# One decoder layer on one core: loads of a second input moved ahead, a gate's small products moved behind larger ones, and the last tile computed half by half

## Chip, core and metric

The kernel runs on one NeuronCore of a Trainium2 chip. The metric is device time of one execution in microseconds (us). A profile is one further execution recorded by the hardware profiler; times inside it count from the start of its span.

## What is computed

One layer of a hybrid decoder for a prompt of 1024 tokens and 8 samples of 4 tokens (32 columns beside the 1024). Cut to what matters here:

```python
u = rmsnorm(x, norm_pre); proj = u @ w_in                  # all mixer inputs and gates
a = hgrn2_branch(...) @ w_pa; b = swa_branch(...) @ w_pb
m = sigmoid(ga) * a + sigmoid(gb) * b
y = m @ w_o
x = x + rmsnorm(y, norm_post)
e = (p @ w_ple) * sigmoid(x @ w_ple_gate)                  # p: the second input, 256 wide
x = x + e
```

The change lies in the last three lines: in how `p` (`p_prompt`, `p_sample`) is loaded and transposed while `m @ w_o` runs, and in `x @ w_ple_gate` with the output that follows it.

## The kernel before, in words

Activations lie with channels on partitions and tokens along the free dimension. A weight matrix of 1024 columns is worked through in four tiles, each of two blocks of 128 output columns (`across`: blocks p and p+4). float32 operands are split in a high and a low part (`wh`, `wl` for weights, H.., L.. for activations), so that one block product takes three matmuls of 128x512.

`pair_gemm` (L403) computes one such tile. For w_pa, w_pb and w_o it uses a seven-product scheme with "plain" groups for the two contraction blocks that are left over: products P1, P5, P6, P3, P7, P2, P4 of 9 matmuls each, and four plain groups (`plain`, L432) of 6, 87 matmuls in all. They accumulate in three PSUM banks (tile name `g`) which rotate. Product P2 takes the bank that the first plain group had filled, and that bank is free only when VectorE has added it into the tile `p5` (L497). P7 reads the activation variant T3, P2 the variant B21, P4 the variant T4. The variants of the next stage's input are made by `build` (L1459) on VectorE and ScalarE during the first tile of that stage: L1487 subtracts, L1488 rounds to the high part, L1489 makes the low part. T4 is the last; it is made in the tile `ts` with buffer tag `t12`.

The 32 sample columns take another way: `sample_products` (L387) multiplies in 16 small matmuls (L391) and copies the result out on ScalarE (`part`, L394); `sample_outputs` (L397) turns it with four small matmuls (L399), which wait for that copy.

The gate's tiles are of kind "plain" (L456): for each of the two blocks (`j`) both token halves (`t`, 512 columns each) are accumulated in two banks, 36 matmuls, then a plain group of 6 for each half. For j = 0 the sample products and the sample outputs stand between the 36 matmuls and the first plain group. After each half `ep_o` (L1713) works on ScalarE (sigmoid, L1717) and VectorE (L1718, L1719), and after the second half `turn_out` (L1694) is queued: transposes on TensorE (`os` for the samples, `op` for four blocks of 128 tokens), a copy on ScalarE (L1706) and the output DMA.

Order of work. TensorE runs in the order in which the program is written; the order on VectorE and ScalarE, and that of the DMAs on the queue of SyncE (SP), is set by a scheduler. Work beside the matmuls is written as generators in queues; `tick` (L213) is called once in so many matmuls (3 in the stages of w_pa, w_pb and w_o, 6 in the gate), advances the first entry of each queue, and a `yield n` lets n ticks pass. A DMA waits on SP in order: what stands behind a DMA whose buffer is not yet free waits too.

`turn_p` (L1568) transposes p. It starts when the variants of `m` are built (that is, written in the program), takes the tile `pw` of six places with the tag `t12` that `ts` had, and for each of nine blocks issues the load, lets four ticks pass, transposes twice on TensorE (`ppp`, L1578), and splits the result (L1581 on ScalarE, L1582 on VectorE).

Of the kernel before, what the change touches and what calls it, by code (L numbers as in the profile page):

```python
# [121 lines left out]
def tile_decoder_step(ctx: ExitStack, tc: tile.TileContext, x_prompt, x_sample, state_hgrn, cache_k, cache_v,  # L122
# [280 lines left out]
    def pair_gemm(W, X, eps, quantum=QUANTUM, late=False):  # L403
# [53 lines left out]
        if W.kind == "plain":  # L457
            for j in range(2):
                ps = [bank(banks[0]), bank(banks[1])]
# [14 lines left out]
                if j == 0:  # L474
                    sample_outputs(gs, part, eps)
                for t in range(2):
                    plain(ps[t], j, t, False)
                    eps[j](HT * t, slice(HT * t, HT * t + HT), ps[t])
# [1089 lines left out]
    def turn_p():  # L1568
        yield until(("built", id(xm)))
        pw = rt.tile([P, 6, 256], F32, name="pw", tag="t12")  # L1570
        for i in range(9):
            r = P if i < 8 else 32
            pt = pw[:, i % 6, :]
            DM.dma_start(pt[:r], p_prompt[0, 0, i * P:(i + 1) * P, :] if i < 8 else p_sample[0].rearrange("b t d -> (b t) d"))
            yield 4
            b = fps.tile([P, 512], F32, name=f"ppp{i}", tag="xp", bufs=3)
            for k in range(2):
                T.transpose(b[:, k * P:k * P + r], pt[:r, k * P:(k + 1) * P], ident[:r, :r])  # L1578
            bv = b[:, :256].rearrange("p (k t) -> p k t", k=2)[:, :, :r]
            sl = slice(i * P, i * P + r)  # L1580
            S.copy(pH[:, :, sl], bv)  # L1581
            V.tensor_tensor(pL[:, :, sl], bv, pH[:, :, sl], op=ALU.subtract)  # L1582

# [110 lines left out]
    def turn_out(i):  # L1694
        on = op_.tile([P, 9, P], F32, name=f"out{i}", tag="out", bufs=3)
        last = i == KT - 1
        for lo, hi in ((8, 9), (0, 4), (4, 8)):
# [7 lines left out]
            else:  # L1705
                S.copy(on[:, lo:hi, :], b.rearrange("p (j c) -> p j c", j=4))  # L1706
                if last or hi == 8:
                    s = lo if last else 0
                    DM.dma_start(y_prompt[0, s * P:hi * P, i * P:(i + 1) * P].rearrange("(n p) c -> p n c", p=P), on[:, s:hi, :])
            yield 1  # L1710

    for p, W in enumerate(gate_pairs):
        def ep_o(i):  # L1713
            def ep_(ci, sl, ps):
                sg = ctile()[:, :ps.shape[-1]]
                e = eS[:, i, :] if ci == NP else eP[i][ci // HT]
# [3 lines left out]
                if ci == HT:  # L1720
                    enqueue(turn_out(i), 2)
            return ep_

        pair_gemm(W, x1, [ep_o(i) for i in across[p]])
# [28 lines left out]
```

## Time and profile before

| | |
|---|---|
| device time, median of 3 runs | 1540.57 us (1536.43 to 1541.49) |
| the profiled execution's own time | 1533.76 us |
| its span, first to last instruction | 1531.7 us |
| TensorE busy | 1480.7 us, 97% |
| VectorE busy | 1131.8 us, 74% |
| ScalarE busy | 737.6 us, 48% |
| DMA | 85 GB/s mean |

The time of the profiled execution is its span and some 2 us around it. TensorE (PE in the rows) is busy nearly throughout, so what counts is where it stands still, and where its clock is lower. Rows name a line of the kernel, the engine, and output<-input; what stands in square brackets is idle time of that engine just before, and who ended it. [...] The stages that matter here: the tiles of w_pb up to 1282 us, of w_o from there to 1381, the projection of p from 1381 to 1415 with the residual beside it, the gate from 1415 on.

### The profile page before, as it was taken

To read this page: it belongs to the slowest core of one execution; us is meant where nothing else is said; L and a number is where in the kernel's file an instruction comes from. 1 tells how busy PE (TensorE), PEld (TensorE's weight loads), DVE (VectorE), ACT (ScalarE), POOL (GpSimd) and SP (SyncE) were. 2 spreads that over 40 slices of the span, in tenths; PEclk is the share of its full clock that TensorE was granted. 3 is DMA by queue.
4 is the path that set the end of the run, shared out by engine and by line. 5 is a ranking of instruction groups with operands and counts; after the bars stand their busy time and mean duration, and the time that the engine had idled before them with its cause. 6 is when DMAs were issued, how large, how long until landed. Compare 5 with 4: busy or idle time off the path is not lost.

```text
span 1531.7 us, 27146 instructions
## 1 busy us (share of the span) xinstructions
PE 1480.7 (97%) x10013; PEld 1168.8 (76%) x10013; DVE 1131.8 (74%) x2627; ACT 737.6 (48%) x1913; POOL 141.5 (9%) x131
## 2 busy tenths in 40 slices
PE   8889999999999999999999999999999997999998
PEld 7767787877778877777777777777777776789776
DVE  7778868686868777776788788875886979547532
ACT  6334444545354444445555555644634426556332
POOL 2243111202020202013000000000000000000000
PEclk9999999999999999999999999999999999999999
DMA  5212131212122121212222211124665621214221
GB/s 188 70 31 84 43 100 42 74 56 85 57 73 70 61 80 45 83 52 69 61 55 64 51 49 49 48 88 145 223 222 164 230 80 49 62 57 119 78 71 57
DMA packets 197999, 129.51 MB, mean 85 GB/s; under 512 B 47075, under 2 KB 185500, under 8 KB 197852
## 3 DMA queue, kind: packets, MB, share of 16 engines
q1 hardware_dynamic: 197052, 127.54, 27.4%
q8 instruction: 79, 1.29, 0.4%
q14 instruction: 52, 0.43, 0.1%
q0 software_dynamic: 672, 0.18, 0.1%
q10 hardware_dynamic: 144, 0.07, 0.0%
HBM read 96.89 MB, written 31.88 MB: 84 GB/s over the span
## 4 chain that ended last, share of the span: by engine, by line
PE 85%; DVE 7%; DMA 3%; ACT 2%; issue 2%; POOL 1%; SPq 1%; ACTq 0%; DVEq 0%; POOLq 0%
PE g L409 63%; PE gs L391 3%; PE po L1264 2%; PE pt L1249 1%; PE g L840 1%; PE gs L399 1%; PE g L1684 1%; PE lp L1217 1%; PE d L1058 1%; PE d L1020 1%; PE lp L1221 1%; PE d L1060 1%; DVE stk L1402 1%; DMA raw<-in_w_in_dram 1%; DMA gb_d<-ct 1%
## 5 line engine op out<-in xcount | busy, mean ns | idle before, releaser
L409 PE MATMUL g<-HT,wh 128*128 128x512 f32 x588 | 241.3, 410 | 3.2 <-DVE ct L453 1.8
L409 PE MATMUL g<-LT,wh 128*128 128x512 f32 x588 | 232.8, 396 | 0.4 <-DVE LT L1489 0.4
L409 PE MATMUL g<-HT,wl 128*128 128x512 f32 x588 | 232.4, 395 | 0.0
L409 PE MATMUL g<-HB,wh 128*128 128x512 f32 x522 | 213.3, 409 | 1.9 <-DVE p L497 1.9
L409 PE MATMUL g<-HB,wl 128*128 128x512 f32 x522 | 205.9, 394 | 0.0
L409 PE MATMUL g<-LB,wh 128*128 128x512 f32 x522 | 205.3, 393 | 0.0
L409 PE MATMUL g<-HR,wrh 128*128 128x512 f32 x416 | 172.3, 414 | 0.0
L289 ACT CAST wh<-ws 128x384 fp32r<-128x384 f32 x184 | 93.7, 512 | 155.9 <-PE g L409 114.6
L409 PE MATMUL g<-HR,wrl 128*128 128x512 f32 x416 | 165.4, 398 | 0.0
L409 PE MATMUL g<-LR,wrh 128*128 128x512 f32 x416 | 164.6, 396 | 0.0
L289 ACT CAST wh<-raw 128x384 fp32r<-128x384 f32 (+1 forms) x170 | 86.5, 510 | 144.6 <-PE g L409 125.6
L290 DVE TENSOR_TENSOR wl<-raw,wh 128x384 fp32r<-128x384 f32 (+1 forms) x170 | 94.2, 556 | 76.9 <-ACT wh L289 76.5
L290 DVE TENSOR_TENSOR wl<-ws,wh 128x384 fp32r<-128x384 f32 x184 | 113.2, 617 | 48.1 <-ACT wh L289 46.7
L409 PEld LDWEIGHTS g<-HT,wh 128*128 128x128 f32 x588 | 110.9, 189 | 46.3 <-ACT c L446 8.3
L409 PEld LDWEIGHTS g<-HT,wl 128*128 128x128 f32 x588 | 110.9, 189 | 24.7 <-issue 0.9
L409 PEld LDWEIGHTS g<-LT,wh 128*128 128x128 f32 x588 | 111.2, 189 | 21.3 <-DVE LT L1489 0.8
L409 PEld LDWEIGHTS g<-HB,wh 128*128 128x128 f32 x522 | 98.2, 188 | 26.6 <-issue 4.3
L409 PEld LDWEIGHTS g<-HB,wl 128*128 128x128 f32 x522 | 98.2, 188 | 22.0 <-issue 0.5
L409 PEld LDWEIGHTS g<-LB,wh 128*128 128x128 f32 x522 | 98.4, 189 | 18.2 <-issue 0.7
L409 PEld LDWEIGHTS g<-HR,wrl 128*128 128x128 f32 x416 | 78.9, 190 | 17.3 <-issue 0.5
L409 PEld LDWEIGHTS g<-HR,wrh 128*128 128x128 f32 x416 | 79.4, 191 | 15.2 <-issue 0.7
L409 PEld LDWEIGHTS g<-LR,wrh 128*128 128x128 f32 x416 | 79.4, 191 | 14.3 <-issue 0.7
(405 smaller groups left out, 2709.7 us busy)
## 6 DMA issues: line engine op xcount, KB each, us to landing
raw<-in_w_in_dram SPq DMA_DIRECT2D x116, 256.0 KB
raw<-in_w_in_dram SPq DMA_DIRECT2D x64, 128.0 KB
oa_d<-G SPq DMA_DIRECT2D x8, 528.0 KB
oar<-oa_d SPq DMA_DIRECT2D x8, 528.0 KB
sga<-ga_d SPq DMA_DIRECT2D x8, 528.0 KB
obr<-ob_d SPq DMA_DIRECT2D x8, 528.0 KB
ma_d<-sga SPq DMA_DIRECT2D x8, 528.0 KB
gbr<-gb_d SPq DMA_DIRECT2D x8, 528.0 KB
```

Of the source, the lines that this page charges most:

```text
L289: S.copy(h, x)
L290: eng.tensor_tensor(l, x, h, op=ALU.subtract)
L391: T.matmul(gs[r, :2 * P], xs[:, k, :], raws[k // 4][:, k % 4].rearrange("p j m -> p (j m)"), start=k < 4, stop=k >= 4, tile_position=(0, 3 ...
L399: T.matmul(gs[:, 256 + 32 * j:288 + 32 * j], part[:, P * j:P * j + P], cst[:, C_S32:C_S32 + 32], start=True, stop=True)
L409: T.matmul(ps, a, b, start=start, stop=stop, skip_group_check=True)
L840: T.matmul(ps, a[:, k, :], b, start=k == 0 and m == 0, stop=k == KT - 1 and m == 2)
L1020: T.matmul(b[:, c * P:(c + 1) * P], kn[:, c, :], vn[:, c, :], start=True, stop=True)
L1058: T.matmul(o, att[:, c, :], vn[:, c, :], start=True, stop=c == 0)
L1060: T.matmul(o, QE[:, c * P:(c + 1) * P], St[:, c - 1, :], start=False, stop=True)
L1217: T.matmul(bs[j][:, os], q3[:, j, qs], KK[j][:, ks], start=w == 0, stop=False, skip_group_check=True)
L1221: T.matmul(bs[j][:, os], q3[r, j, qs], KL[r, ks], start=False, stop=w == 1, skip_group_check=True, tile_position=(64 * j, 0))
L1264: T.matmul(po[r, lo:hi], vN[:, kb, r], pT[:, j, lo:hi], start=i == 0, stop=i == len(items) - 1, skip_group_check=True, tile_position=(0, 6 ...
```

## The change

Three edits, in the places that the diff shows.

1. `turn_p` issues the first six loads at once, lets 24 ticks pass, and then transposes a block every four ticks; the loads of blocks 6 to 8 are issued behind the transposes of blocks 0 to 2, whose places in `pw` they take.
2. In the gate's tiles `sample_outputs` is written behind the plain group of the first token half instead of before it.
3. In the last tile (`x1.last`), the second block computes the first token half to its end and then the second, each in one bank; the second half's sigmoid, product, sum, transposes, copy and output go in two pieces of 256 tokens. `turn_out` takes its pieces as an argument, is queued once for each piece of the last block, and each piece of four (or two) token blocks has an output DMA of its own for every tile, where before seven of the eight tiles had one DMA for both.

```diff
@@ -456,6 +456,23 @@
 
         if W.kind == "plain":
             for j in range(2):
+                if j == 1 and X.last:
+                    for i in range(2):
+                        prepared()
+                    for t in range(2):
+                        ps = bank(banks[0])
+                        banks.append(banks.pop(0))
+                        for i in range(2):
+                            wh, wl = W.v[i, j]
+                            xh, xl = X.v[(("T3", "B11"), ("B22", "B21"))[i][t]]
+                            for k in range(M):
+                                for m, (a, b) in enumerate(((wh, xh), (wh, xl), (wl, xh))):
+                                    mm(ps, a[:, k, :], b[:, k, :], i + k + m == 0, not R and i == 1 and k == M - 1 and m == 2)
+                        plain(ps, j, t, False)
+                        w = HT // (1 + t)
+                        for lo in range(0, HT, w):
+                            eps[j](HT * t + lo, slice(HT * t + lo, HT * t + lo + w), ps[:, lo:lo + w])
+                    continue
                 ps = [bank(banks[0]), bank(banks[1])]
                 banks.append(banks.pop(0))
                 banks.append(banks.pop(0))
@@ -471,10 +488,10 @@
                 if j == 0:
                     wait_for("s")
                     gs, part = sample_products(W.raw, X.s)
-                if j == 0:
-                    sample_outputs(gs, part, eps)
                 for t in range(2):
                     plain(ps[t], j, t, False)
+                    if j == 0 and t == 0:
+                        sample_outputs(gs, part, eps)
                     eps[j](HT * t, slice(HT * t, HT * t + HT), ps[t])
             tick()
             return
@@ -1568,11 +1585,16 @@
     def turn_p():
         yield until(("built", id(xm)))
         pw = rt.tile([P, 6, 256], F32, name="pw", tag="t12")
+
+        def fetch(i):
+            DM.dma_start(pw[:P if i < 8 else 32, i % 6, :], p_prompt[0, 0, i * P:(i + 1) * P, :] if i < 8 else p_sample[0].rearrange("b t d -> (b t) d"))
+
+        for i in range(6):
+            fetch(i)
+        yield 24
         for i in range(9):
             r = P if i < 8 else 32
             pt = pw[:, i % 6, :]
-            DM.dma_start(pt[:r], p_prompt[0, 0, i * P:(i + 1) * P, :] if i < 8 else p_sample[0].rearrange("b t d -> (b t) d"))
-            yield 4
             b = fps.tile([P, 512], F32, name=f"ppp{i}", tag="xp", bufs=3)
             for k in range(2):
                 T.transpose(b[:, k * P:k * P + r], pt[:r, k * P:(k + 1) * P], ident[:r, :r])
@@ -1580,6 +1602,9 @@
             sl = slice(i * P, i * P + r)
             S.copy(pH[:, :, sl], bv)
             V.tensor_tensor(pL[:, :, sl], bv, pH[:, :, sl], op=ALU.subtract)
+            if i + 6 < 9:
+                fetch(i + 6)
+            yield 4
 
     def eps_o(i):
 
@@ -1691,10 +1716,13 @@
     op_, _ = opened("op", side="right")
     ctx.enter_context(_)
 
-    def turn_out(i):
-        on = op_.tile([P, 9, P], F32, name=f"out{i}", tag="out", bufs=3)
-        last = i == KT - 1
-        for lo, hi in ((8, 9), (0, 4), (4, 8)):
+    outs_ = {}
+
+    def turn_out(i, chunks):
+        if i not in outs_:
+            outs_[i] = op_.tile([P, 9, P], F32, name=f"out{i}", tag="out", bufs=3)
+        on = outs_[i]
+        for lo, hi in chunks:
             b = fps.tile([P, 512], F32, name=f"op{i}_{lo}", tag="xp", bufs=3) if lo < 8 else fps.tile([P, 512], F32, name=f"os{i}", tag="sm", bufs=1)
             for q in range(lo, hi):
                 o = b[:, (q - lo) * P:(q - lo + 1) * P] if q < 8 else b[:32, :P]
@@ -1703,24 +1731,27 @@
                 V.tensor_copy(on[:32, 8, :], b[:32, :P])
                 DM.dma_start(y_sample.rearrange("b t d -> (b t) d")[:, i * P:(i + 1) * P], on[:32, 8, :])
             else:
-                S.copy(on[:, lo:hi, :], b.rearrange("p (j c) -> p j c", j=4))
-                if last or hi == 8:
-                    s = lo if last else 0
-                    DM.dma_start(y_prompt[0, s * P:hi * P, i * P:(i + 1) * P].rearrange("(n p) c -> p n c", p=P), on[:, s:hi, :])
+                S.copy(on[:, lo:hi, :], b[:, :(hi - lo) * P].rearrange("p (j c) -> p j c", c=P))
+                DM.dma_start(y_prompt[0, lo * P:hi * P, i * P:(i + 1) * P].rearrange("(n p) c -> p n c", p=P), on[:, lo:hi, :])
             yield 1
 
     for p, W in enumerate(gate_pairs):
         def ep_o(i):
             def ep_(ci, sl, ps):
-                sg = ctile()[:, :ps.shape[-1]]
-                e = eS[:, i, :] if ci == NP else eP[i][ci // HT]
+                w = ps.shape[-1]
+                sg = ctile()[:, :w]
+                e = eS[:, i, :] if ci == NP else eP[i][ci // HT][:, ci % HT:ci % HT + w]
                 S.activation(sg, ps, AF.Sigmoid)
                 V.tensor_tensor(e, e, sg, op=ALU.mult)
                 V.tensor_tensor(yT[i][:, sl], yT[i][:, sl], e, op=ALU.add)
-                if ci == HT:
-                    enqueue(turn_out(i), 2)
+                if i < KT - 1:
+                    if ci == HT:
+                        enqueue(turn_out(i, ((8, 9), (0, 4), (4, 8))), 2)
+                elif ci < NP:
+                    enqueue(turn_out(i, ((8, 9), (0, 4)) if ci == 0 else ((ci // P, ci // P + 2),)), 2)
             return ep_
 
+        x1.last = p == KT // 2 - 1
         pair_gemm(W, x1, [ep_o(i) for i in across[p]])
     drain()
```

How it moves instructions, at three places. The names: g is a PSUM bank, with the number that tells one filling from another; HB, LB, HT, LT, HR, LR are variants of the activations, wh, wl, wrh, wrl weights, raw a loaded weight tile, gs the sample products, xs the sample columns, ppp the transposes of p.

First place, TensorE in the first tile of w_o, before: the transposes of the first block of p stand behind the 9 matmuls of product P3.

```order
L409 MATMUL g_13719<-LB_13605,wh_13691 128x512
L409 MATMUL g_13719<-HB_13604,wl_13692 128x512
L1578 MATMUL ppp_13823<-cst,pw 128x128 x2
L409 MATMUL g_13719<-HR_13674,wrh_13651 128x512
L409 MATMUL g_13719<-LR_13675,wrh_13651 128x512
L409 MATMUL g_13719<-HR_13674,wrl_13652 128x512
```

Now the plain group follows P3 directly, then P7, P2 and P4 with theirs, and the transposes come in the second tile, behind its sample products:

```order
L391 MATMUL gs_13933<-raw_13619,xs_13595 32x256 x4
L391 MATMUL gs_13933<-raw_13743,xs_13595 32x256 x4
L409 MATMUL g_13946<-HT_13517,wh_13859 128x512
L409 MATMUL g_13946<-LT_13518,wh_13859 128x512
L409 MATMUL g_13946<-HT_13517,wl_13860 128x512
L1600 MATMUL ppp_13954<-cst,pw 128x128 x2
L409 MATMUL g_13946<-HT_13517,wh_13859 128x512
```

The first transposes moved back by 54 matmuls of 128x512 and the second tile's sample products.

The same place on SP's queue, before (raw_13743 is the last weight load that was issued ahead of p; raw_13870 to raw_14201 are those of the third and fourth tile):

```order
L246 DMA raw_13743<-in_w_o_dram 128x4x128 x2
L1574 DMA pw<-in_p_prompt_dram 128x256 x3
L246 DMA raw_13870<-in_w_o_dram 128x4x128 x2
L1574 DMA pw<-in_p_prompt_dram 128x256 x5
L1574 DMA pw<-in_p_sample_dram 32x256
L246 DMA raw_13997<-in_w_o_dram 128x4x128 x2
L246 DMA raw_14097<-in_w_o_dram 128x4x128 x2
L246 DMA raw_14201<-in_w_o_dram 128x4x128 x2
```

and now:

```order
L246 DMA raw_13743<-in_w_o_dram 128x4x128 x2
L1590 DMA pw<-in_p_prompt_dram 128x256 x6
L246 DMA raw_13863<-in_w_o_dram 128x4x128 x2
L246 DMA raw_13972<-in_w_o_dram 128x4x128 x2
L1590 DMA pw<-in_p_prompt_dram 128x256 x2
L246 DMA raw_14072<-in_w_o_dram 128x4x128 x2
L1590 DMA pw<-in_p_sample_dram 32x256
L246 DMA raw_14201<-in_w_o_dram 128x4x128 x2
```

Six loads of p instead of three stand ahead of the third tile's first weights, and three that wait for transposes stand among the weights of the third and fourth tile. On VectorE the order from the building of the variants to the sum into p5 is what it was.

Second place, TensorE at the end of the first block in the gate's second tile, before:

```order
L391 MATMUL gs_15310<-raw_14864,xs_14522 32x256 x4
L391 MATMUL gs_15310<-raw_14990,xs_14522 32x256 x4
L399 MATMUL gs_15310<-cst,part_15319 128x32 x2
L409 MATMUL g_15243<-HR_15076,wrh_15156 128x512
L409 MATMUL g_15243<-LR_15077,wrh_15156 128x512
```

and now:

```order
L391 MATMUL gs_15312<-raw_14864,xs_14522 32x256 x4
L391 MATMUL gs_15312<-raw_14990,xs_14522 32x256 x4
L409 MATMUL g_15244<-HR_15076,wrh_15156 128x512
L409 MATMUL g_15244<-LR_15077,wrh_15156 128x512
L409 MATMUL g_15244<-HR_15076,wrl_15157 128x512
L409 MATMUL g_15244<-HR_15076,wrh_15156 128x512
L409 MATMUL g_15244<-LR_15077,wrh_15156 128x512
L409 MATMUL g_15244<-HR_15076,wrl_15157 128x512
L399 MATMUL gs_15312<-cst,part_15321 128x32 x2
```

Six matmuls moved in between the sample products and the sample outputs, as in each of the gate's four tiles.

Third place, VectorE at the very end, before (e is the product with the sigmoid, y the result, os the transposed samples):

```order
L1718 TENSOR_TENSOR e_14520<-e_14520,ct_15805 128x512
L1719 TENSOR_TENSOR y_14404<-y_14404,e_14520 128x512
L1703 COPY out_15819<-os_15820 32x128
L1718 TENSOR_TENSOR e_14521<-e_14521,ct_15815 128x512
L1719 TENSOR_TENSOR y_14404<-y_14404,e_14521 128x512
```

and now:

```order
L1745 TENSOR_TENSOR e_14520<-e_14520,ct_15793 128x512
L1746 TENSOR_TENSOR y_14404<-y_14404,e_14520 128x512
L1731 COPY out_15816<-os_15817 32x128
L1745 TENSOR_TENSOR e_14521<-e_14521,ct_15834 128x256
L1745 TENSOR_TENSOR e_14521<-e_14521,ct_15838 128x256
L1746 TENSOR_TENSOR y_14404<-y_14404,e_14521 128x256 x2
```

The second half's product and sum became two of 256 each, both products ahead of both sums; the samples' transposes now stand on TensorE ahead of the last six matmuls, and their copy with them.

## Rows read from the trace of the kernel before

**Rows 1.** The waits of TensorE from 700 us to the end, longest in total first: total us, times, the longest.

```profile
PE ppp L1578 <- DMA pw<-in_p_prompt_dram: 8.3, 1, 8.3
...
PE gs L399 <- ACT part L394: 1.9, 4, 0.5
PE g L409 <- DVE p L497: 1.9, 1, 1.9
PE g L409 <- DVE ct L453: 1.8, 1, 1.8
```

**Rows 2.** TensorE in order of time in the first tile of w_o: start, us, instruction.

```profile
1291.09 0.40 PE L409 MATMUL g<-HB,wh 128*128 128x512 f32 x1
...
1292.92 0.39 PE L409 MATMUL g<-HB,wl 128*128 128x512 f32 x1
1301.64 0.69 PE L1578 MATMUL ppp<-cst,pw 128*128 128x128 f32 x2 [8.33 <-DMA pw<-in_p_prompt_dram]
1301.98 0.78 PE L409 MATMUL g<-HR,wrh 128*128 128x512 f32 x1
...
1305.54 0.40 PE L409 MATMUL g<-HT,wl 128*128 128x512 f32 x1
```

**Rows 3.** VectorE in order of time at the same place.

```profile
1292.26 1.89 DVE L1489 TENSOR_TENSOR LT<-ct,HT 128x512 fp32r<-128x512 f32 x3
...
1297.68 1.89 DVE L1489 TENSOR_TENSOR LT<-ts,HT 128x512 fp32r<-128x512 f32 x3
...
1299.59 0.68 DVE L497 TENSOR_TENSOR p<-g,p 128x512 f32<-128x512 f32 x1
```

**Rows 4.** DMA issues on SP's queue from 1287 to 1342 us: start, us from the first to the last of them.

```profile
1299.59 0.82 SPq L1574 DMA_DIRECT2D pw<-in_p_prompt_dram  x2
...
1300.99 0.93 SPq L246 DMA_DIRECT2D raw<-in_w_o_dram  x2
```

**Rows 5.** TensorE in order of time at the same point of the first tile of w_pb, the stage before.

```profile
1208.85 0.50 PE L409 MATMUL g<-HB,wh 128*128 128x512 f32 x1 [1.94 <-DVE p L497]
...
1209.65 0.40 PE L409 MATMUL g<-HB,wh 128*128 128x512 f32 x1
...
1213.52 0.39 PE L409 MATMUL g<-LR,wrh 128*128 128x512 f32 x1
```

**Rows 6.** VectorE in order of time at that point.

```profile
1208.12 0.68 DVE L497 TENSOR_TENSOR p<-g,p 128x512 f32<-128x512 f32 x1
```

**Rows 7.** Stretches (from:to, length, busy us of PE, PEld, DVE, ACT and POOL with instructions, granted clock, DMA share, GB/s): behind the wait of rows 5, in the wait of rows 2 and behind it, and around the wait of 1.8 us that VectorE's L453 ends (rows 1).

```profile
1209.80:1213.40 3.60, 3.60 (x11) 2.81 (x10) 3.60 (x9) 0.00 (x0) 0.00 (x0) 0.53 0.88 255
...
1293.30:1301.70 8.40, 0.07 (x2) 0.06 (x1) 8.37 (x16) 2.31 (x6) 0.00 (x0) 0.62 0.12 33
1301.70:1305.50 3.80, 3.80 (x10) 3.07 (x11) 1.56 (x3) 0.37 (x1) 0.00 (x0) 0.50 0.93 273
...
1078.00:1082.00 4.00, 2.20 (x10) 1.52 (x9) 2.85 (x6) 1.23 (x2) 0.00 (x0) 1.00 0.98 319
```

**Rows 8.** TensorE and ScalarE in order of time at the samples of the gate's second tile.

```profile
1455.34 1.07 PE L391 MATMUL gs<-raw,xs 128*32 128x256 f32 x16
...
1456.48 0.37 ACT L394 COPY part<-gs 128x256 f32<-128x256 f32 x1 [4.58 <-PE gs L391]
1456.90 0.63 PE L399 MATMUL gs<-cst,part 128*128 128x32 f32 x4 [0.49 <-ACT part L394]
1457.37 0.48 PE L409 MATMUL g<-HR,wrh 128*128 128x512 f32 x1
```

**Rows 9.** The same instructions in a tile of w_o, where other matmuls already stand between the two (start, us).

```profile
1339.75 1.07 PE L391 MATMUL gs<-raw,xs 128*32 128x256 f32 x16
...
1340.75 0.50 PE L409 MATMUL g<-HT,wh 128*128 128x512 f32 x1
...
1345.01 0.53 PE L399 MATMUL gs<-cst,part 128*128 128x32 f32 x4
...
1345.37 0.48 PE L409 MATMUL g<-HR,wrh 128*128 128x512 f32 x1
```

**Rows 10.** The end of the span on all engines in order of time.

```profile
1524.15 0.39 PE L409 MATMUL g<-HR,wrl 128*128 128x512 f32 x1
...
1524.58 0.60 ACT L1717 ACTIVATE ct<-g 128x512 f32<-128x512 f32 x1 [0.76 <-PE g L409]
1525.19 0.27 DVE L1703 COPY out<-os 32x128 f32<-32x128 f32 x1
...
1525.39 0.67 DVE L1718 TENSOR_TENSOR e<-e,ct 128x512 f32<-128x512 f32 x1
...
1526.09 0.69 DVE L1719 TENSOR_TENSOR y<-y,e 128x512 f32<-128x512 f32 x1
1526.69 1.89 SPq L1709 DMA_DIRECT2D out_dram<-out  x2
...
1526.93 0.63 PE L1701 MATMUL op<-cst,y 128*128 128x128 f32 x4 [0.89 <-DVE y L1719]
1527.60 0.59 ACT L1706 COPY out<-op 128x512 f32<-128x512 f32 x1 [0.93 <-PE op L1701]
```

**Rows 11.** Instructions by line, engine and shape with busy us and mean ns of one: pieces of 256 columns, from 1290 to 1340 us.

```profile
L1582 DVE TENSOR_TENSOR pL<-ppp,pH 128x256 fp32r<-128x256 f32 x8 | 3.4, 422 | 5.6 <-ACT pH L1581 5.6
L1581 ACT CAST pH<-ppp 128x256 fp32r<-128x256 f32 x8 | 2.9, 367 | 6.6 <-PE ppp L1578 6.6
```

## Prediction, made blind

> **What bounds the kernel now.** I read the page first: TensorE is busy 97% of the span, so the time can only fall where it waits, where its clock is down, or after its last matmul. The list of its waits from 700 us on has one that stands out: 8.3 us, once, for the first load of p [rows 1]. Further down come 1.9 us in four waits of the sample outputs for ScalarE's copy, and two single waits for VectorE of 1.9 and 1.8 us [rows 1]. Then I read the timelines there, engine by engine, to see what would come next if a wait went away, and last the end of the span.
>
> In the first tile of w_o, TensorE starts the last matmul of product P3 at 1292.92 and then stands until 1301.64 [rows 2]. SP's queue issued the load only at 1299.59 [rows 4], because its buffer had belonged to T4, whose last low part VectorE starts at 1297.68 and ends at 1299.57 [rows 3]. The load took two more us. So the wait is a full VectorE first and a load second. When TensorE goes on, eight matmuls take from 1301.98 to 1305.54 [rows 2], at a granted clock of 0.50, the 1.2 GHz level; within the wait it was 0.62 on the mean, with next to no work on TensorE [rows 7].
>
> **Edit 1, the loads of p.** *What it removes:* the wait of 8.33 us. The pitch of matmuls here is (1292.92 - 1291.09) / 8 = 0.229 us [rows 2], so without the transposes the plain group would start at 1293.15 instead of the transposes at 1301.64: 8.49 us.
>
> *What comes next there.* The plain group (6 matmuls) needs nothing new. P7 (9) reads T3, whose three low parts run from 1292.26 to 1294.15 [rows 3]; P7 would start at 1293.15 + 6 x 0.229 = 1294.52, just behind. P2 would start 9 pitches later, at 1296.58. But P2 needs the bank that L497 empties, and L497 stands on VectorE behind T4, from 1299.59 to 1300.27 [rows 3]; the change leaves that order as it is. VectorE shows no idle time there, so a TensorE that comes earlier doesn't make it earlier. The same place exists in w_pb, without any load of p: L497 from 1208.12 to 1208.80 [rows 6], P2 at 1208.85 after an idle time of 1.94 us [rows 5]. So P2 starts at 1300.32, and a new wait of 1300.32 - 1296.58 = 3.74 us, counted from start to start (about 3.6 as idle time), replaces the 8.49. That gives 4.75 us.
>
> *The clock.* Before, the eight matmuls took 3.56 us instead of 8 x 0.229 = 1.83, and the transposes ahead of them some 0.2 more than later ones: 1.9 us lost. After the w_pb wait of 1.94 us the clock also fell, to 0.53 in the stretch behind it [rows 7], and ten matmuls took from 1209.65 to 1213.52, 3.87 instead of 2.29: 1.6 us lost [rows 5]. After the 1.8 us wait the granted clock stayed 1.00 in the stretch [rows 7]. The new wait is twice as long as the one after which the clock fell, so I take one such loss, 1.6. The clock then gives 0.3 back. Its ends: no fall, 1.9 back; twice as many matmuls at the low level, 1.3 lost.
>
> *What it moves.* The nine pairs of transposes with their ScalarE and VectorE work are the same number, later; each still costs TensorE its own time. Their loads now have 24 ticks of 3 matmuls, some 16 us, and wait no longer. On SP six loads at 0.41 each [rows 4] stand ahead of the third tile's first weights, 2.5 us instead of three loads' 1.2, so these weights come 1.2 us later in a tile that begins some 25 us later: nothing. Loads 6 and 7 of p wait for the transposes of blocks 0 and 1 with the fourth tile's weights behind them; these wait for later work anyway. The ones for the norm (tag `t12`) now wait on VectorE for the ninth pair, which stands early in the third tile; behind it are that tile's weights, needed 36 matmuls later: nothing. Edit 1 in sum: 4.75 + 0.3 = 5.0 us, between 3.4 and 6.6.
>
> **Edit 2, the sample outputs.** Before, from the start of the sample products to the next plain matmul it is 1457.37 - 1455.34 = 2.03 us: TensorE stands 0.46 us for the copy at 1456.48 [rows 8]. In w_o, where matmuls already lie between, the products take 1340.75 - 1339.75 = 1.00 and the outputs 1345.37 - 1345.01 = 0.36 [rows 9]. So 2.03 - 1.36 = 0.67 us in each tile. The cover is six matmuls, 1.37 us, over a copy that ends 0.4 us after the products. The first tile waits for the copy as well (four waits in all, [rows 1]), so four times: 2.7 us. If the first tile gains nothing, since it hangs on the residual's last steps, it is 2.0; that is the low end, 2.9 the high one. *The added wait:* on ScalarE the two sigmoids of the samples now stand ahead of that of the first half, which comes about 0.8 us later; its bank is taken again only after 6 + 9 matmuls, 3.4 us. Covered.
>
> **Edit 3, the last tile.** From the end of the last matmul (1524.15 + 0.39) to the end of the span at 1531.7 it is 7.16 us: sigmoid 0.60, 0.2 in which VectorE is held by the copy of `os`, product 0.67, sum 0.69, transposes 0.63, copy 0.59, issue 0.37, landing 3.12 [rows 10]. In pieces of 256, a VectorE operation takes 0.42 and a ScalarE one 0.37 [rows 11]. With E for the end of the last matmul: the sigmoids run from E + 0.04 to 0.74, the two products to 1.2, the sums, back to back behind them as the new order has them, to 1.55 and 1.9; the last two transposes end at 2.45, their copy at 2.85, the issue at 3.25. With 3.12 for the landing again that is E + 6.36, 0.8 less. The piece is half as large, so the landing may be shorter by up to 0.4; the transposes of `os` now lie before E and cost 0.1. I take 0.8, between 0.5 and 1.2.
>
> [...]
>
> The other output DMAs become fourteen instead of seven, of half the size, on a queue that has hardly anything else to do there. I cost them at nothing; that is a rival, below.
>
> **Sum.** 5.0 + 2.7 + 0.8 = 8.5 us; lowest 3.4 + 2.0 + 0.5 = 5.9, highest 6.6 + 2.9 + 1.2 = 10.7. Against the profiled execution's own time of 1533.76 that is 1525.3. That execution lies 6.8 us below the median of the runs, which I can't explain by a row; the gain should be the same in both, so 1540.57 - 8.5 = 1532.1.
>
> **The rivals.**
>
> *The clock stays up at the new wait.* For it: it stayed up over the 1.8 us wait [rows 7]. Against: the new wait is twice that. It gives 1.6 more: 1530.5.
>
> *The clock is down longer.* For it: the longer wait of rows 2 cost 1.9, the shorter one of rows 5 1.6, so the loss may grow with the wait, and nothing here shows a wait between them. Against: from 1.94 to 8.33 us of idle time it grew by only 0.3. With twice as many matmuls at the low level it costs another 1.6: 1533.7.
>
> *The wait only moves.* TensorE comes earlier to a VectorE that has no slack, and after P2 it meets the next things that VectorE owes it: the sum that empties P4's bank, the second tile's weights. By VectorE's order that sum comes four operations after L497; at 0.68 us each, as L497, it ends at 1300.27 + 2.7 = 1303.0, and P4 needs it at 1300.32 + 15 x 0.229 = 1303.8: 0.8 us of slack. If these waits ate all of edit 1, 3.5 us would be left: 1537.1, within 0.3%.
>
> *Slower, by the output DMAs.* Place: the gate's output tiles, of which there are three; ScalarE's copy into one waits for the DMAs that read it before. Price: the last DMA takes 3.12 us from issue to landing; seven more of them, if waited for, cost 22 us, and the time would be 1540.57 - 8.5 + 22 = 1554. It decides when a DMA lands later than its tile is needed again, three blocks or some 40 us after. So there is far too much room. [...] No run here has such a wait.
>
> **How the numbers follow.** Forecast 0.60 (1532.1); clock stays up 0.13 (1530.5); clock down longer 0.10 (1533.7); the wait only moves 0.13 (1537.1); slower 0.04. About 0.3%, 4.6 us, is what a measurement of this kernel can tell from no change. The first three are faster by more: 0.83; the fourth is the same: 0.13; slower 0.04. The range takes the runs' own spread in: the lowest run less the highest gain, 1536.43 - 10.7 = 1525.7, and the highest run less the lowest gain, 1541.49 - 5.9 = 1535.6, to which I add a little for the fourth case: 1525.7 to 1536.6.
>
> **What would show it.** Right: no wait on a load of p; one wait of 3.5 to 3.8 us ahead of P2 in w_o's first tile, ended by L514 (L497 before), with a stretch at 1.2 GHz behind it; no wait of the sample outputs for the copy in the gate; 6.0 to 6.6 us from the last matmul to the end. Wrong: a second wait before P4 or in the second tile, a wait on weights in the third or fourth, a wait of ScalarE's copies for output DMAs, or P2 starting clearly earlier than L497 allows.

## The result, and the profile after

The changed kernel takes 1526.18 us (median of 4 runs, 1525.09 to 1527.76), the kernel before on the same basis 1539.47 us (4 runs, 1536.43 to 1541.49). The ratio is 0.9917, 95% interval 0.9902 to 0.9932: faster by 0.83%, or 12.8 us (10.5 to 15.1). The forecast was 8.5 us. A second set of six runs of the changed kernel gave 1526.10 us and a ratio of 0.9920.

The three places that the forecast spoke of look as it said. First TensorE's waits of the profile after, from 700 us to the end (line, tile, what was waited for: us in total, times, longest). L514 is the L497 of before:

```profile
PE g L409 <- DVE p L514: 5.5, 2, 3.6
...
PE g L409 <- DVE ct L453: 2.0, 1, 2.0
PE op L1729 <- DVE y L1746: 1.3, 1, 1.3
```

Against [rows 1] the wait on a load of p is gone, and so are the sample outputs' waits for ScalarE's copy. One new wait of 3.61 us stands ahead of P2 in w_o's first tile. TensorE's timeline there (start, duration, instruction, idle time and what ended it), to be held against [rows 2]:

```profile
1295.68 0.39 PE L409 MATMUL g<-HT,wl 128*128 128x512 f32 x1
1299.68 0.80 PE L409 MATMUL g<-HB,wh 128*128 128x512 f32 x1 [3.61 <-DVE p L514]
1300.28 0.63 PE L409 MATMUL g<-LB,wh 128*128 128x512 f32 x1
...
1304.97 0.44 PE L409 MATMUL g<-HR,wrh 128*128 128x512 f32 x1
1305.24 0.40 PE L409 MATMUL g<-LR,wrh 128*128 128x512 f32 x1
```

VectorE's timeline beside it, as in [rows 3]: the sum follows T4's low parts without a gap.

```profile
1297.04 1.89 DVE L1506 TENSOR_TENSOR LT<-ts,HT 128x512 fp32r<-128x512 f32 x3
1298.84 0.19 DVE L1622 TENSOR_TENSOR acc<-acc,ct 128x32 f32<-128x32 f32 x1
1298.94 0.69 DVE L514 TENSOR_TENSOR p<-g,p 128x512 f32<-128x512 f32 x1
```

TensorE alone in three stretches there (its busy time, count, granted clock as a share of the full one, DMA share, GB/s): within the wait, behind it, and after that.

```profile
1297.00:1299.60 2.60, 0.00 (x0) 0.73 0.00 0
1299.70:1305.00 5.30, 5.30 (x13) 0.50 0.83 247
1305.30:1311.00 5.70, 5.70 (x27) 1.00 0.00 1
```

A granted clock of 0.50 is what the forecast calls the 1.2 GHz level: the 128x512 matmuls start 0.426 us apart there (1300.28 to 1304.97, 11 pitches), 1.2 columns per ns. The matmuls from 1299.68 to 1305.24, 13 pitches, took 5.56 us instead of 13 x 0.229 = 2.98: the clock cost 2.6 us here, where 1.6 was forecast.

The gate, second tile, TensorE, to be held against [rows 8]: the outputs now come after six plain matmuls, without a wait.

```profile
1450.45 1.07 PE L391 MATMUL gs<-raw,xs 128*32 128x256 f32 x16
1451.45 0.50 PE L409 MATMUL g<-HR,wrh 128*128 128x512 f32 x1
1451.80 0.40 PE L409 MATMUL g<-LR,wrh 128*128 128x512 f32 x1
...
1452.96 0.53 PE L399 MATMUL gs<-cst,part 128*128 128x32 f32 x4
1453.33 0.48 PE L409 MATMUL g<-HR,wrh 128*128 128x512 f32 x1
```

The end of the span, all engines, to be held against [rows 10]:

```profile
1517.95 0.39 PE L409 MATMUL g<-HR,wrl 128*128 128x512 f32 x1
...
1518.38 0.66 ACT L1744 ACTIVATE ct<-g 128x256 f32<-128x256 f32 x2 [4.96 <-PE g L409]
1518.80 0.76 DVE L1745 TENSOR_TENSOR e<-e,ct 128x256 f32<-128x256 f32 x2 [1.51 <-ACT ct L1744]
...
1519.48 0.75 DVE L1746 TENSOR_TENSOR y<-y,e 128x256 f32<-128x256 f32 x2
...
1520.49 0.71 ACT L1734 COPY out<-op 128x256 f32<-128x256 f32 x2 [0.97 <-PE op L1729]
```

From the last matmul's end, 1518.34, to the end of the span at 1524.39 it is 6.05 us; before it was 1531.65 - 1524.54 = 7.11 (the forecast's 7.16 took the rounded 1531.7).

**Where the time came from, stretch by stretch.** Every pair of weight tiles has one group of sample products (L391), so their 53 starts cut the trace at the same places in every kernel. Summed into stretches (us), for two profiles of each kernel (the second ones are from the experiments below):

| stretch | before | before, 2nd | after | after, 2nd |
|---|---|---|---|---|
| start to the first pair | 52.4 | 52.3 | 53.0 | 51.8 |
| head 0 | 79.7 | 79.8 | 76.8 | 76.6 |
| the other heads, k and v | 594.1 | 594.2 | 594.1 | 594.1 |
| attention, gate b's first half | 336.3 | 337.7 | 337.8 | 337.9 |
| rest of gate b, w_pa, w_pb | 221.5 | 222.6 | 221.7 | 221.6 |
| w_o, tiles 1 to 3 | 77.2 | 77.2 | 73.2 | 73.2 |
| w_o's last tile, norm, w_ple | 66.6 | 66.5 | 66.7 | 66.8 |
| gate, to the last matmul | 96.7 | 98.6 | 95.0 | 95.0 |
| to the end of the span | 7.1 | 7.1 | 6.0 | 6.0 |
| span | 1531.7 | 1536.0 | 1524.4 | 1523.1 |

What the forecast named is there: w_o 4.0, the gate 1.7 or more, the end 1.1. What it did not name is **head 0**: 3 us.

### The profile page after: what moved, and what is told of

Same layout as the page of the kernel before. It is cut to its first block, busy times and chain, and to the rows that moved or that the text cites. A ratio compares the mean times of both kernels' runs of the same rounds, so it can differ in the third digit from the quotient of the medians.

```text
span 1524.4 us, 27176 instructions
## 1 busy us (share of the span) xinstructions
PE 1482.5 (97%) x10013; PEld 1170.1 (77%) x10013; DVE 1126.6 (74%) x2629; ACT 736.9 (48%) x1915; POOL 143.6 (9%) x131
## 4 chain that ended last, share of the span: by engine, by line
PE 84%; DVE 7%; DMA 3%; issue 2%; ACT 2%; POOL 1%; SPq 0%; ACTq 0%; DVEq 0%; POOLq 0%
PE g L409 63%; PE gs L391 3%; PE po L1281 2%; PE pt L1266 1%; PE g L857 1%; PE g L1709 1%; PE gs L399 1%; DMA raw<-in_w_in_dram 1%; PE d L1075 1%; PE lp L1234 1%; PE d L1077 1%; PE lp L1238 1%; PE d L1037 1%; DVE stk L1419 1%; DMA xt<-in_x_prompt_dram 1%
## 5 line engine op out<-in xcount | busy, mean ns | idle before, releaser
L409 PEld LDWEIGHTS g<-HB,wl 128*128 128x128 f32 x522 | 98.6, 189 | 22.2 <-issue 0.5
```

The lines of the kernel that those rows point to most:

```text
L409: T.matmul(ps, a, b, start=start, stop=stop, skip_group_check=True)
```

## The experiments

All times are medians, each beside runs of the kernel before on the same chip (1538.7 us in the first four, 1538.2 in the next four, 1536.9 in the three after that, 1538.8 in the last). Gains in us are (1 - ratio) x that median, with the interval's ends.

**One edit at a time.** The kernel before with the new `turn_p` alone:

```diff
+        for i in range(6):
+            fetch(i)
+        yield 24
...
-            yield 4
```

> The kernel before with edit 1 alone (six loads of p ahead, 24 places). Theory (the forecast's steps, with the clock loss that the profile of after shows, 2.5 us instead of 1.6): 4 to 5 us less than the kernel before, with one wait of about 3.6 us ahead of P2 in w_o's first tile, ended by L514, and 1.2 GHz behind it. Rival (the part of the gain between the medians that the two profiles don't show, some 5 us, belongs to the loads): 9 to 10 us less.

Measured: 1533.39 us, ratio 0.9964 (0.9952 to 0.9976): 5.5 us less (3.7 to 7.4). The wait of 3.6 us is there, the granted clock from 1250 to 1320 us is 0.95 as in the changed kernel (0.93 before), and w_o's first three tiles take 73.2 us against 77.2. The theory's 4 to 5 lies in the interval, the rival's 9 doesn't.

Edit 2 alone:

```diff
-                if j == 0:
-                    sample_outputs(gs, part, eps)
                 for t in range(2):
                     plain(ps[t], j, t, False)
+                    if j == 0 and t == 0:
+                        sample_outputs(gs, part, eps)
```

> The kernel before with edit 2 alone (sample outputs behind the first plain group of a gate tile). Theory: 2.0 to 2.9 us less, no wait of the sample outputs for ScalarE's copy. Rival (the unexplained 5 us belong to the gate): 7 to 8 us less.

Measured: 1530.45 us, ratio 0.9958 (0.9943 to 0.9973): 6.5 us less (4.2 to 8.8). The theory's 2.0 to 2.9 is refuted. The rival had the size, but not the place: most of it lies in head 0. Its second and third pairs are marked `plain` as well (line 1090 of the kernel before), and the list of waits from 700 us on couldn't show it. The same list over the whole span of the kernel before has 6.2 us in seven waits where [rows 1] have 1.9 in four:

```profile
PE gs L399 <- ACT part L394: 6.2, 7, 3.2
```

TensorE at the second pair in the kernel before:

```profile
64.69 1.07 PE L391 MATMUL gs<-raw,xs 128*32 128x256 f32 x16
69.00 0.63 PE L399 MATMUL gs<-cst,part 128*128 128x32 f32 x4 [3.24 <-ACT part L394]
...
70.09 0.63 PE L409 MATMUL g<-HR,wrl 128*128 128x512 f32 x1
70.51 0.63 PE L409 MATMUL g<-HR,wrh 128*128 128x512 f32 x1
```

ScalarE there: the copy stands in its queue behind a cast that waits for VectorE.

```profile
68.05 0.62 ACT L559 CAST HT<-ct 128x512 fp32r<-128x512 f32 x1 [8.94 <-DVE ct L558]
68.58 0.37 ACT L394 COPY part<-gs 128x256 f32<-128x256 f32 x1
```

And TensorE with edit 2 alone:

```profile
64.28 1.07 PE L391 MATMUL gs<-raw,xs 128*32 128x256 f32 x16
65.28 0.50 PE L409 MATMUL g<-HR,wrh 128*128 128x512 f32 x1
...
68.64 0.63 PE L399 MATMUL gs<-cst,part 128*128 128x32 f32 x4 [1.71 <-ACT part L394]
69.11 0.48 PE L409 MATMUL g<-HR,wrh 128*128 128x512 f32 x1
69.42 0.40 PE L409 MATMUL g<-LR,wrh 128*128 128x512 f32 x1
69.65 0.39 PE L409 MATMUL g<-HR,wrl 128*128 128x512 f32 x1
```

The copy comes at the same time in both, 3.89 and 3.94 us after the first sample product. Six matmuls now lie in the wait, so it is 1.71 instead of 3.24, and the matmuls behind it run at the full clock (0.23 apart) instead of the low one (0.43).

Edit 3 alone (the plain branch for `X.last` and `turn_out` with its chunks, as in the diff of the change):

```diff
+                if j == 1 and X.last:
...
+                        w = HT // (1 + t)
```

> The kernel before with edit 3 alone (last tile's halves in turn, second half in two pieces). Theory: 0.5 to 1.2 us less, and 6.0 to 6.6 us from the end of the last matmul to the end of the span. Rival (the unexplained 5 us belong to the tail or to the output loads' order): 5 to 6 us less. If all three parts give what the theory says, their sum is 7 to 9 us and the rest of the difference between the medians is between executions, not in the change.

Measured: 1538.41 us, ratio 0.9996 (0.9984 to 1.0009): 0.6 us less (-1.4 to 2.5). The timing can't tell so little; the profile has 6.0 us at the end instead of 7.1. The three parts give 5.5 + 6.5 + 0.6 = 12.6 us, the whole 12.8: within the intervals they add up, and the unexplained share was mostly edit 2's.

**Edit 2 in two halves.** In head 0 alone, and in the gate alone:

```diff
-                if j == 0:
+                if j == 0 and X.made is not None:
                     sample_outputs(gs, part, eps)
...
+                    if j == 0 and t == 0 and X.made is None:
+                        sample_outputs(gs, part, eps)
```

(the gate's kernel has the two conditions exchanged).

> The kernel before with edit 2 in one tile only: the second pair of head 0, which is also of the plain kind and which the forecast did not count. Theory (the first runs: from this tile's sample products to the third tile after them it is 67.4 us without edit 2, and 62.9, 64.4 or 67.4 with it, by how often the clock falls there): 3 to 4.5 us less than the kernel before. Rival (the unforeseen part of edit 2 is a spread between executions): under 1.5 us less.

> The kernel before with edit 2 in the gate's four tiles only, the part that the forecast did count. Theory: 0.48 us a tile by the profiles, 1.9 us less than the kernel before (the forecast said 2.7, at least 2.0). Rival (the gate alone carries all of edit 2's 6 us): 6 us less.

Measured: head 0 alone 1534.86 us, ratio 0.9977 (0.9965 to 0.9989), 3.5 us less (1.7 to 5.4). Gate alone 1536.50 us, ratio 0.9981 (0.9967 to 0.9996), 2.9 us less (0.6 to 5.1). Together 6.4, as edit 2 alone. Both theories hold; the gate's 1.9 and 2.9 can't be told apart. TensorE's waits from 50 to 130 us, in the kernel before:

```profile
PE gs L399 <- ACT part L394: 4.2, 3, 3.2
PE d L982 <- DVE QE L988: 3.8, 1, 3.8
...
```

and with edit 2 in head 0 alone:

```profile
PE d L1060 <- DVE S L1048: 2.6, 1, 2.6
PE gs L399 <- ACT part L394: 2.2, 2, 1.7
PE d L800 <- DVE K L989: 1.6, 1, 1.6
PE d L979 <- DVE attD L996: 1.1, 1, 1.1
```

The edit reaches the third pair of head 0 too, where a wait of 0.49 us for the copy is gone; the expectation speaks of one tile only. Part of the gain is given back in head 0 itself: other waits for VectorE come later in it.

The profiles divide the gain in two. From the sample products of head 0's second pair to those of head 1's first, TensorE stands idle for 8.9 to 9.0 us in all six profiles without edit 2 and for 7.2 to 7.4 in all eight with it: 1.7 us less. The rest goes by the clock:

| that stretch | mean granted clock | profiles |
|---|---|---|
| without edit 2, 67.4 to 67.5 us | 0.95 | five |
| without edit 2, 68.6 us | 0.93 | one |
| with edit 2, 62.9 us | 1.00 | one (edit 2 alone) |
| with edit 2, 64.4 to 64.5 us | 0.97 | four (the changed kernel's two among them) |
| with edit 2, 66.1 us | 0.95 | one |
| with edit 2, 67.3 to 67.4 us | 0.92 | two (edit 2 in head 0 alone is one) |

So in its one profile edit 2 in head 0 alone gains only 0.1 us in that stretch; its 3.5 us stand on the medians of its runs.

**Distance or head start.** The first load 28 places ahead of its transposes, the others one by one as before:

```diff
-            yield 4
+            yield 4 if i else 28
```

> The kernel before with the first load of p 28 places ahead of its transposes and the others one at a time, 4 places ahead, as they were: the distance of edit 1 without the six loads ahead. Theory (only the first load was waited for, and the distance covers it): the same as edit 1 alone, 4 to 5 us less than the kernel before, with no wait on a load of p. Rival (the later loads need the head start): waits of 1 us or more on loads of p, and less than 3 us gained.

Measured: 1533.42 us, ratio 0.9959 (0.9942 to 0.9976), 6.3 us less (3.7 to 8.9), no wait on a load of p, 73.4 us in w_o's three tiles. The distance does all of edit 1; the six loads ahead add nothing that shows.

**The new wait.** Two ways to take T4 from in front of the sum L514. First its differences and low parts on GpSimd, which is idle there:

```diff
-                    V.tensor_tensor(s, p, q, op=ALU.subtract)
+                    (G if n == "T4" else V).tensor_tensor(s, p, q, op=ALU.subtract)
                 S.copy(h, s)
-                V.tensor_tensor(l, s, h, op=ALU.subtract)
+                (G if n == "T4" else V).tensor_tensor(l, s, h, op=ALU.subtract)
```

> The changed kernel, with T4's three differences and three low parts on GpSimd instead of VectorE, in all three stages that build their next operand. Theory (the wait ahead of P2 is VectorE's T4 standing ahead of the sum that empties the bank): six operations of some 0.6 us leave VectorE, 3.6 us, so the 3.61 us wait goes or falls under 0.5, the granted clock stays up, and w_o's first tile alone gives 3.6 + 2.5 = 6 us; with the same wait in w_pb, 6 to 9 us less than the changed kernel. Rival (the wait only moves: T4's operations take 1.5 us each on GpSimd, 9 us in a row, so P4 waits for them instead of P2): 0 to 2 us less, with a wait on P4 ended by GpSimd. A second rival, that GpSimd slows VectorE beside it: VectorE operations longer than 0.69 us there.

Measured: 1529.10 us, ratio 0.9943 (0.9929 to 0.9956), 3 to 4 us more than the changed kernel (by the medians, on different chips, or by the ratios). P2's wait in w_o fell from 3.61 to 1.58, w_pb's stayed at 1.88, and w_o's first tile from 27.9 to 24.1 us; but the tile before it rose from 21.5 to 25.2, gate b's last (gate b is `gb`, the second gate of the mixer) from 21.5 to 23.3 and w_pa's first from 22.2 to 23.1; w_pb's first, 23.7 to 25.3, has the old wait, and from 1100 to 1250 us the mean granted clock is 0.99 instead of 1.00. TensorE has no wait there that GpSimd ended, so the first rival falls. In the tile before w_o TensorE now waits 1.89 us for VectorE's L453, and behind it matmuls start 0.43 us apart (1285.14 to 1288.13, seven pitches) instead of 0.23. The second rival's reason shows there, where both engines work at once:

```profile
1278.15 3.34 POOL L1504 TENSOR_TENSOR ts<-m,ts 128x512 f32<-128x512 f32 x2 [65.91 <-DVE LT L1506]
1278.55 0.68 DVE L453 TENSOR_TENSOR ct<-g,u 128x512 f32<-128x512 f32 x1
1279.15 1.19 DVE L1504 TENSOR_TENSOR ts<-m,ts 128x512 f32<-128x512 f32 x1
1280.26 1.79 DVE L1567 TENSOR_TENSOR gbr<-gbr,ct 128x512 f32<-128x512 f32 x1
```

VectorE's two operations on SBUF take 1.19 and 1.79 beside GpSimd instead of 0.69; L453, one of whose inputs is PSUM (`g`), keeps its 0.68.

Second, the sum earlier in VectorE's queue. The sample outputs force all of the build to be written out (`ep_` ticks until it is built), so they are put behind the sum:

```diff
         product(a, "P6", "T2", False)
-        sample_outputs(gs, part, eps)
+        if not late:
+            sample_outputs(gs, part, eps)
         u2 = kept("u2", a)
...
                 V.tensor_tensor(p5, b, p5, op=ALU.add)
+                sample_outputs(gs, part, eps)
```

> The changed kernel, with the sample outputs behind the sum that empties P2's bank in the late tiles, so that this sum stands on VectorE ahead of most of T3, B21 and T4 instead of behind them. Theory (P2 waits for the sum's place on VectorE, not for its operands): P2's wait of 3.61 us goes; P4 then waits up to 2.4 us for VectorE, whose work ahead of P4's bank is the same; 2.3 to 3.9 us less in w_o's first tile, up to 2 more in w_pb's. Rival (the wait only moves, and the clock falls behind it as before): P4 waits as long as P2 did, and the time is within 1 us of the changed kernel's.

Measured: 1523.58 us, ratio 0.9901 (0.9883 to 0.9919). VectorE does the sum 7.65 us after the tile's first sample products (1289.62 - 1281.97), where it was 15.58 (1298.94 - 1283.36), and P2 doesn't wait. TensorE in w_o's first tile:

```profile
1300.51 0.53 PE L409 MATMUL g<-HT,wh 128*128 128x512 f32 x1 [2.40 <-DVE ct L453]
1300.84 0.63 PE L409 MATMUL g<-LT,wh 128*128 128x512 f32 x1
```

P4 waits 2.40 us, which is the 2.4 of the expectation, and the tile takes 25.8 us instead of 27.9: 2.1 less, a little under the 2.3 to 3.9 expected; w_pb's first tile gives 0.5. The whole is 2.5 to 2.9 us less than the changed kernel, by the ratios and the medians. So the sum's place in the queue was the cause, and VectorE's work is next.

Then the sum that empties P4's bank is put ahead of the other half's:

```diff
         product(a, "P7", "T3", False)
-        out(1, 0, a, p5)
+        if late:
+            d1, d0 = ctile(), ctile()
+            V.tensor_tensor(d1, a, p5, op=ALU.add)
+            V.tensor_tensor(d0, c, u2, op=ALU.add)
+            eps[0](0, slice(0, HT), d0)
+            eps[1](0, slice(0, HT), d1)
...
```

> The kernel with the sum that empties P2's bank first (e8), and in its late tiles also the sum that empties P4's bank ahead of the sum of the other weight half. Theory (P4 waits for that sum's place on VectorE): one operation of 0.6 us less ahead of it, so P4's wait in w_o's first tile falls from 2.40 to 1.8 us, and the two others ended by that sum by 0.6 each; 1 to 2 us less than e8 in three places, 1.6 more for each place where the clock then stays up. Rival (VectorE's total is the bound, and the sum put behind is waited for next): the same waits under another line, within 0.5 us of e8.

Measured: 1519.18 us (four runs, 1518.14 to 1520.39), ratio 0.9878 (0.9858 to 0.9899); the changed kernel on that chip had 1526.10 (1523.87 to 1526.17). **This beats both kernels**, by 1.2% and 0.45%. TensorE in w_o's first tile, and the stretches within and behind that wait (busy time of PE, PEld, DVE, ACT, POOL, granted clock, DMA share, GB/s):

```profile
1298.44 0.47 PE L409 MATMUL g<-HT,wh 128*128 128x512 f32 x1 [1.80 <-DVE ct L528]
```

```profile
1296.70:1298.40 1.70, 0.00 (x0) 0.00 (x0) 1.70 (x5) 0.07 (x1) 0.00 (x0) 1.00 0.29 85
1298.50:1303.00 4.50, 4.50 (x20) 3.75 (x21) 3.95 (x8) 4.50 (x10) 0.00 (x0) 1.00 0.82 253
```

L528 is the sum that empties P4's bank. One operation earlier, the wait is 1.80 instead of 2.40, and in this profile the clock stays up: 23.9 us for the tile. The two other waits that L453 ended fell by more than the 0.6 expected: in w_pb's first tile from 1.47 to 0.37, and in the tile at 1062 us, 2.31 before, only 0.35 for ScalarE is left. By the ratios it is 3.5 us less than with the first sum alone; the expectation had 1 to 2, and 1.6 more for each place where the clock then stays up, and the profiles show that for w_o's first tile: 1.00 behind the wait, 0.53 behind the one of 2.40 (1300.6 to 1304.0 us).

**The end in one piece.** The second token half whole:

```diff
-                        w = HT // (1 + t)
+                        w = HT
...
-                    enqueue(turn_out(i, ((8, 9), (0, 4)) if ci == 0 else ((ci // P, ci // P + 2),)), 2)
+                    enqueue(turn_out(i, ((8, 9), (0, 4)) if ci == 0 else ((ci // P, ci // P + 4),)), 2)
```

> The changed kernel, with the last tile's second token half in one piece of 512 instead of two of 256. Theory (the split pays because the second piece's steps overlap the first's; the halves in turn alone take away only the copy of the sample outputs, 0.2 us): from the end of the last matmul to the end of the span 6.7 to 7.0 us instead of 6.05, and the time 0.7 to 0.9 us more than the changed kernel. [...]

Measured: 1526.07 us, ratio 0.9924 (0.9906 to 0.9943), not to be told from the changed kernel's 0.9920 on the same chip. The profile tells it: the last matmul ends at 1516.59 (1516.20 + 0.39), the span at 1523.63, so 7.0 us. The last steps of it:

```profile
1518.83 0.63 PE L1729 MATMUL op<-cst,y 128*128 128x128 f32 x4 [1.79 <-DVE y L1746]
1519.49 0.59 ACT L1734 COPY out<-op 128x512 f32<-128x512 f32 x1 [1.79 <-PE op L1729]
```

From the last matmul's end to the end of that copy it is 3.49 us, and in two pieces 1521.20 - 1518.34 = 2.86. The split gives 1.0 us, 0.6 of it up to the copy; for the rest, the span ends 3.19 us after that copy, whose output is half as large, instead of 3.55. Halves in turn without the split give 0.1 (7.1 to 7.0).

**Both kernels once more.**

> The changed kernel unchanged, on the same chip as the two above, as what they are to be compared with, and for a second profile of it. Theory (which waits the clock falls behind differs from execution to execution in head 0 and at the waits of 1.8 to 2 us, and not at the wait of 3.6 us): tile by tile the same times as in the first profile, but for 1.4 to 1.8 us in some of the tiles with such waits; in w_o's first tile 27.9 us again. Rival (the code sets where the clock falls): the same tiles slow in both profiles.

> The kernel before unchanged, for a second profile of it. The forecast could not explain that its profiled execution (1533.76 us) lies 6.8 us below the median of its runs. Theory (the clock falls at a handful of short waits in one execution and not in the next): the second profile's time lies nearer to the median, and tile by tile it differs from the first by 1.4 to 1.8 us at a time, in tiles with such waits. Rival (something else is slower outside profiles): the same span as the first, within 1 us, and the same tiles slow.

Measured: after 1526.10 us with a profile of 1525.26; before 1538.90 us (ratio 1.0007, 0.9990 to 1.0024) with a profile of 1538.09, near the median, where the first had 1533.76. The second profile of before is 4.3 us longer in few places: tiles around 755 us 1.5, the tile at 1062 us 2.8, the first gate tile 1.8, w_pb's first tile -1.6. That last one is [rows 5] over again, the same wait, but here the clock stays up:

```profile
1213.01 0.50 PE L409 MATMUL g<-HB,wh 128*128 128x512 f32 x1 [1.94 <-DVE p L497]
1213.35 0.39 PE L409 MATMUL g<-LB,wh 128*128 128x512 f32 x1
1213.58 0.40 PE L409 MATMUL g<-HB,wl 128*128 128x512 f32 x1
```

Not all of it is the clock, whose mean is 0.988 in the second profile and 0.992 in the first. In the tile at 1062 us TensorE's wait for L453 is 1.80 and 3.17 us in the two profiles of before, since VectorE itself waited 0.85 and 2.22 there for a store of gate b to give back its buffer. Changed against before, second profiles, the table above has 1536.0 - 1523.1 = 12.9 us, close to the 12.8 of the runs; the first two have 7.3, so one pair of profiles doesn't settle such a difference. The rival of a fixed set of slow tiles falls for before. The two profiles of after agree within 0.2 us in every stretch but the first (53.0, with a granted clock of 0.89 from 0 to 30 us, and 51.8); at 1080 us the first has the low clock behind a wait of 1.97 us (matmuls 0.43 us apart), and the second a longer wait without it (0.23 apart):

```profile
1080.09 0.50 PE L409 MATMUL g<-HT,wh 128*128 128x512 f32 x1 [3.47 <-DVE ct L453]
```

## Why the forecast was right, and where not

**Edit 1.** The wait removed, the one in its place and its cause were as forecast: from 1295.68 + 0.229 to 1299.68 it is 3.77 us, against 3.74. Mis-sized was the clock's term: "I take one such loss, 1.6" was 2.6 here. So edit 1 gives 8.49 + 1.9 - 3.77 - 2.6 = 4.0 instead of 5.0, within its bounds, and the table's 77.2 - 73.2 says the same. In the four profiles of the changed part besides this one, w_o's first tile took 27.8 to 28.0 three times and 27.0 once.

**Edit 2** has the step that failed: "each tile ... so four times: 2.7 us". It counted the gate's four tiles, because the waits were read from 700 us on and the code that sets `kind` wasn't followed to head 0. There edit 2 gives 3.5 us by the runs (1.7 to 5.4); 1.7 us of idle time goes in every profile, and the clock, 0.92 to 1.00 on the mean of that stretch with the edit, adds to it or takes it back. The four that were counted give 0.48 each in the profiles, 1.9 in all, a little under the low end of 2.0: outputs and products take 1.00 and 0.37 as forecast, but the first plain matmul behind the products has a pitch of 0.35 instead of 0.23, and there is one such place more.

**Edit 3** gives 1.1 us at the end, where 0.8 was forecast, within its bounds. The chain up to the last copy came as forecast, 2.86 us after the last matmul against 2.85; the difference lies behind it, in issue and landing, 3.19 us against 3.52; the forecast had left the landing at the whole piece's 3.12, with up to 0.4 less as a possibility. The pieces aren't free: a product or sum of 256 takes 0.42 us at the changed kernel's end, two in a row 0.76 and 0.75, where the whole took 0.67 and 0.69 [rows 10]. The split still paid 1.0.

**The sum** was 8.5, the runs say 12.8 (10.5 to 15.1). With head 0's 3.5 in it, 4.0 + 1.9 + 1.1 + 3.5 = 10.5, the interval's low end. The remaining 2 are within what the clock does from one execution to the next (head 0's stretch with edit 2 takes 62.9 us at a mean of 1.00 and 67.3 to 67.4 at 0.92); which waits carry them is not settled. The measured gain lies above the forecast's highest, 10.7. That the time, 1526.2 us, still lies in the range is luck in part: the range also took in the spread of the runs of the kernel before, and its low end, 1525.7, is only 0.5 below. The point, 1532.1, lay 5.9 us too high.

**The rivals.** The clock did not stay up at the new wait; it stayed low for 13 pitches, more than in [rows 5], though not for 1.6 us more. The wait did not only move: P4 and the second tile show none. No copy of ScalarE waited for an output DMA. Of the unexplained 6.8 us between profile and median, some 2 were the median of three runs (later ones have 1536.9 to 1538.9); the rest was that execution, which missed some falls of the clock (mean 0.992, in the second profile 0.988) and a late store (VectorE waited 0.85 us for it, in the second 2.22): the second profile is 4.3 us longer.

## What to carry to other kernels

Before an edit to a shared routine is costed, list every caller that reaches the edited branch, and read the waits of the whole span: the longest wait that edit 2 shortened stands at 69 us, in the first tenth of it. When an engine waits for a bank, look at where the emptying operation stands in the other engine's queue: moving two sums gave 7 us, and moving the work to an idle engine lost 3 to 4. Take a second profile of the same kernel before a stretch of low clock, or its absence, is put into a sum.

## What the runs showed of the hardware

The clock can fall behind a wait in one execution and not in the next: behind w_pb's 1.94 us it was 0.53 in the first profile of before [rows 7], and in the second the matmuls there start 0.23 us apart; behind 2.40 us in one kernel it was 0.53 and behind 1.80 in another 1.00, and behind 3.47 in the tile at 1062 us in the second profile of after the matmuls start 0.23 apart. With the 3.6 us ahead of P2 it was 0.50 behind the wait in the changed kernel, and w_o's first tile takes 27.0 to 28.0 us in all five profiles that have this wait, where 27.9 - 2.6 = 25.3 is an estimate for the full clock. So no length of wait is shown from which it falls.
